# Down stage of a hybrid attention block: order of plain and seven-product groups, and the banks of the second block

## The chip, the cores and the metric

The kernel runs on one core of a Trainium2 chip. The metric is the device time of one execution in microseconds (us), the median of several runs. A profile of one execution goes with it. PE is TensorE (matmuls), PEld its weight loads, DVE is VectorE, ACT is ScalarE, POOL is GpSimd, SP is SyncE, which here only issues DMAs.

## The reference

One layer of a transformer block on 256 tokens of width 2048, all in float32. Three attention branches, their gated sum and a projection come first; then a feed-forward part. The change touches only the last product, the "down" product:

```python
h2 = rms_norm(x, g_ffn[l])
u = causal_depthwise_conv(h2 @ w_up[l], conv_w[l], conv_b[l])
u_gate, u_val = jnp.split(u, 2, axis=-1)
x = x + (jax.nn.silu(u_gate) * u_val) @ w_down[l]
```

The activations are 256 x 5632 and `w_down` is 5632 x 2048.

## The kernel before

**Three passes for one product.** Every float32 operand is held as a high part and a low remainder (`hi`, `lo`). A product of two such operands is three matmuls (`three`, lines 927 to 930): high by high, low by high, high by low. For the weights, ACT makes `hi` by a copy that rounds (L923), and DVE makes `lo` by a subtraction (L924), in `parts`. There are four `hi` and four `lo` buffers, so a piece of weights can be split only when the piece four earlier has been used up by PE.

**The down stage.** The 2048 output columns are done in two blocks of 1024 (`nb` 0 and 1). In each, the 5632 inner rows are 44 chunks of 128, taken two at a time as 22 groups, numbered `p`. The output of a block is 2 row halves (`t`) by 2 column halves of 512 (`n`), so four accumulators of one PSUM bank each, called `X`. A group is done in one of two ways:

- A plain group, "e" in the plan, function `eight`: eight products of 128 x 128 by 128 x 512, that is 24 matmuls, all into `X`. It takes two steps, one for each chunk. The last group of a block defers its matmuls to its second step and does them accumulator by accumulator (`close`), so that the first accumulator is final 18 matmuls before the last.
- A group by seven products, "s" in the plan, function `seven`: a two by two block product formed with seven products instead of eight, that is 21 matmuls. It takes four steps (`u0` to `u3`). Three products go into `X`, four go into four more accumulators called `Y`, one bank each. It needs sums of the activations (`forms`, lines 882 to 904) and sums of the weights. One part of the weight sums is made during the up stage by `weight_sums` (four loads of 256 KB, three additions on DVE, one write of 512 KB to a scratch tensor `T`, for each seven group); the other is made on the spot by two DVE additions (L985, L986).

After the last seven group of a block, `gather` adds the four `Y` in the right combinations to the residual tiles `xr` (eight DVE additions and one ACT copy, in three portions, the first held back by two further steps). After the block's last step, `finish` issues whatever of `gather` is still open, and `results` adds the four `X` banks to `xr` (L1059) and stores them (L1060).

**The order of the work.** `PLANS` holds one string for each block. In every step the program first issues the preparation of the step two ahead (loads, `hi`, `lo`), then the matmuls of this step, then what was put behind the step, and then one `tick` of the generators (`forms`, `gather`). The DVE, ACT and SP instructions that matter are pinned in this order (`keep`). The activation sums for group number `p` of the sevens are begun by a plain group: in the first block the fourth plain group begins the sums for seven number 0, the fifth those for number 1, and so on; in the second block this goes on from the second plain group. Their three portions are issued behind the plain group's first step, its second step and the step after it.

**The banks.** The first block takes its eight accumulators as four pairs from the pool `pp2` of the up stage. `start(1)` closes that pool and opens `pp3` with eight single banks. The variables `pairs_made`, `first_pair` and `turn_by` rotate the list of these eight before the first four become `X` and the last four `Y`. A bank is tied to a tile at the tile's first use, in the order of first use, and a fresh pool gives out its places from 0 downwards and round: 0, 7, 6, 5, 4, 3, 2, 1. In the program as compiled, the first block's `X` are in banks 0, 1, 6, 7 and its `Y` in 2, 3, 4, 5; the second block's `X` are in 0, 7, 6, 5 and its `Y` in 4, 3, 2, 1. Two tiles of a pair become free together, when both have been read for the last time.

## Time and profile before

| | us |
|---|---|
| median of 3 runs | 1492.92 |
| lowest, highest | 1491.57, 1492.92 |
| the profiled execution | 1492.96 |
| its span, first to last instruction | 1491.0 |

| part of the span | from, to (us) | PE busy | DVE busy | ACT busy | DMA, GB/s |
|---|---|---|---|---|---|
| attention, projections, nearly all of the up stage | 0 to 1250 | 1247.67 | 831.54 | 723.33 | 216 |
| end of the up stage | 1250 to 1256 | 6.00 | 2.63 | 2.34 | 238 |
| first block of the down stage | 1256 to 1372 | 114.69 | 107.40 | 72.17 | 246 |
| second block of the down stage | 1372 to 1491 | 114.18 | 99.19 | 61.74 | 234 |

Between the span and the profiled execution's own time lie 1.96 us. [...] The profile has one value for the clock that TensorE was granted, by stretch of time.

### The profile page before, as it was taken

Reading aid. Unit: us, or ns where it says so; the run is one execution under the profiler, and the core shown is the slowest. Engines: PE = TensorE matmul, PEld = TensorE weight load, DVE = VectorE, ACT = ScalarE, POOL = GpSimd, SP = SyncE. Lnnn points to the kernel's source line nnn. Section 1 sums busy time; section 2 is a strip of 40 time slices with the busy share of each in tenths; the row PEclk is TensorE's granted clock in tenths of the full one; section 3 lists DMA queues with packets and bytes.
Section 4 is the critical chain, followed back from the end, with each engine's and each line's share of the span. In section 5 each row is a group of like instructions: output and inputs, shape, how many; then the busy total and the mean of one; then the engine's idle time right before and its main releaser. Section 6 shows DMA issues by size and latency. Waiting matters only on the chain. (4 is left out here: it accounts for less than half of the span.)

```text
span 1491.0 us, 20205 instructions
## 1 busy us (share of the span) xinstructions
PE 1482.5 (99%) x7411; PEld 1250.9 (84%) x7411; DVE 1040.8 (70%) x1336; ACT 859.6 (58%) x1227; POOL 40.5 (3%) x90
## 2 busy tenths in 40 slices
PE   9999999999999999999999999999999999999998
PEld 7888888888888888888888888888888888887887
DVE  5767566555655646556556887777787787998987
ACT  6755454458544444444456676676676677564654
POOL 1000000001000000000000000000000000001000
PEclk9999999999999999999999999999999999999999
DMA  8675475475676667666677778778877885777874
GB/s 292 187 206 156 128 225 156 120 232 149 191 201 201 194 202 209 193 192 201 211 215 225 246 252 278 244 252 281 259 253 265 267 258 181 243 269 244 284 262 166
DMA packets 155939, 327.70 MB, mean 220 GB/s; under 512 B 11360, under 2 KB 19856, under 8 KB 155840
## 3 DMA queue, kind: packets, MB, share of 16 engines
q1 hardware_dynamic: 150496, 309.95, 66.8%
q0 software_dynamic: 4592, 15.41, 2.9%
q8 instruction: 58, 0.95, 0.3%
q10 hardware_dynamic: 752, 1.06, 0.2%
q14 instruction: 41, 0.34, 0.1%
HBM read 312.21 MB, written 14.16 MB: 219 GB/s over the span
## 5 line engine op out<-in xcount | busy, mean ns | idle before, releaser
L841 PE MATMUL u<-hT,hi_u 128*128 128x512 f32 x1408 | 442.4, 396 | 0.1
L843 PEld LDWEIGHTS u<-hT,lo_u 128*128 128x128 f32 x1408 | 264.4, 188 | 62.8 <-DVE lo_u L147 0.3
L843 PE MATMUL u<-hT,lo_u 128*128 128x256 f32 x1408 | 276.8, 278 | 0.0
L147 DVE TENSOR_TENSOR lo_u<-raw_u,hi_u 128x1024 fp32r<-128x1024 f32 x176 | 212.1, 1220 | 80.3 <-ACT hi_u L146 78.1
L146 ACT CAST hi_u<-raw_u 128x1024 fp32r<-128x1024 f32 x176 | 180.9, 1048 | 115.6 <-DMA raw_u<-in_w_up_dram 58.8
L841 PEld LDWEIGHTS u<-hT,hi_u 128*128 128x128 f32 x1408 | 214.3, 189 | 0.5 <-issue 0.5
L147 DVE TENSOR_TENSOR lo_g<-raw_g,hi_g 128x1024 fp32r<-128x1024 f32 x96 | 117.6, 1227 | 101.4 <-ACT hi_g L146 97.6
L146 ACT CAST hi_g<-raw_g 128x1024 fp32r<-128x1024 f32 x96 | 100.8, 1052 | 121.8 <-PE g L158 98.2
L157 PE MATMUL g<-hi_g,xT 128*128 128x512 f32 x384 | 150.9, 393 | 0.0
L159 PE MATMUL g<-lo_g,xT 128*128 128x512 f32 x384 | 149.6, 390 | 0.0
L158 PE MATMUL g<-hi_g,xT 128*128 128x512 f32 x384 | 149.5, 389 | 0.0
L159 PEld LDWEIGHTS g<-lo_g,xT 128*128 128x128 f32 x384 | 72.1, 188 | 15.2
L157 PEld LDWEIGHTS g<-hi_g,xT 128*128 128x128 f32 x384 | 72.1, 188 | 14.6
L158 PEld LDWEIGHTS g<-hi_g,xT 128*128 128x128 f32 x384 | 72.2, 188 | 14.5
L928 PE MATMUL d<-hi_d,aT 128*128 128x512 f32 x200 | 78.6, 393 | 2.0 <-DVE xr L1059 2.0
L930 PE MATMUL d<-lo_d,aT 128*128 128x512 f32 x200 | 78.5, 392 | 0.0
L929 PE MATMUL d<-hi_d,aT 128*128 128x512 f32 x200 | 78.4, 392 | 0.0
L772 DVE TENSOR_TENSOR y<-y,z 128x512 f32<-128x512 f32 x88 | 60.6, 690 | 20.2 <-ACT z L771 16.7
L771 ACT ACTIVATE z<-u,taps 128x256 f32<-128x256 f32 x176 | 74.7, 496 | 0.0
L147 DVE TENSOR_TENSOR lo_s<-raw_s,hi_s 128x1024 fp32r<-128x1024 f32 (+1 forms) x40 | 44.7, 1118 | 37.2 <-ACT hi_s L146 37.1
L147 DVE TENSOR_TENSOR lo_f<-raw_f,hi_f 128x1024 fp32r<-128x1024 f32 (+1 forms) x40 | 44.7, 1119 | 34.5 <-ACT hi_f L146 33.0
L146 ACT CAST hi_f<-raw_f 128x1024 fp32r<-128x1024 f32 (+1 forms) x40 | 38.6, 968 | 52.3 <-PE f L158 47.6
(332 smaller groups left out, 2801.0 us busy)
## 6 DMA issues: line engine op xcount, KB each, us to landing
raw_u<-in_w_up_dram SPq DMA_DIRECT2D x176, 512.0 KB, 4.6
raw_g<-in_w_in_dram SPq DMA_DIRECT2D x96, 512.0 KB, 4.0
raw_d<-in_w_down_dram SPq DMA_DIRECT2D x50, 512.0 KB, 5.1
r<-in_w_down_dram SPq DMA_DIRECT2D x76, 256.0 KB, 6.2
raw_s<-in_w_down_dram SPq DMA_DIRECT2D x38, 512.0 KB, 5.2
raw_f<-in_w_in_dram SPq DMA_DIRECT2D x32, 512.0 KB, 3.7
raw_s<-in_w_in_dram SPq DMA_DIRECT2D x32, 512.0 KB, 3.7
raw_o<-in_w_out_dram SPq DMA_DIRECT2D x32, 512.0 KB, 4.7
```

Of the source, the lines that this page charges most:

```text
L146: pin(nc.scalar.copy(hi[:, :m], raw[:, :m]))
L147: pin(nc.vector.tensor_tensor(lo[:, :m], raw[:, :m], hi[:, :m].bitcast(F32), ALU.subtract))
L157: nc.tensor.matmul(o, lhsT=xh, rhs=wh, start=first, stop=False)
L158: nc.tensor.matmul(o, lhsT=xl, rhs=wh, start=False, stop=False)
L159: nc.tensor.matmul(o, lhsT=xh, rhs=wl, start=False, stop=last)
L771: nc.scalar.activation(z[:, i], u[:, i, j : j + S], AF.Copy, scale=taps_of(j, i))
L772: nc.vector.tensor_tensor(y, y, z, ALU.add)
L841: nc.tensor.matmul(ps, lhsT=hi[:, j, c], rhs=hT[:, k + j, :], start=first, stop=False)
L843: nc.tensor.matmul(ps[:, :S], lhsT=lo[:, j, c], rhs=hT[:, k + j, :S], start=False, stop=last)
L928: nc.tensor.matmul(o, lhsT=ah, rhs=w[0], start=first, stop=False)
L929: nc.tensor.matmul(o, lhsT=al, rhs=w[0], start=False, stop=False)
L930: nc.tensor.matmul(o, lhsT=ah, rhs=w[1], start=False, stop=last)
```

## The change

Four things in the down stage:

1. The first block's plan keeps its 8 seven groups and 14 plain groups but orders them differently: two seven groups are drawn forward, and three plain groups in a row end the block.
2. The second block's plan has 12 seven groups and 10 plain groups, where it had 11 and 11. Four times two seven groups stand next to each other, and one plain group less lies between.
3. The rotation of the bank list is gone. In its place `start(1)` writes one column of the tiles 4, 5 and 6 with DVE, which are the second block's `Y[0]`, `Y[1]` and `Y[2]`.
4. `start` is called at other places in the program's text; the order in which it runs relative to `finish` and `results` stays.

With one more seven group `NSEVEN` becomes 8 and 12, so `weight_sums` runs 20 times during the up stage instead of 19.

```diff
-PLANS = ("eeeee" + "se" * 7 + "see", "e" + "se" * 4 + "sse" + "se" * 3 + "ssee")
+PLANS = ("eeeee" + "se" * 5 + "sse" + "s" + "eee", "e" + "se" * 3 + "sse" * 4 + "see")
...
-    pairs_made = [0]
-
     def two_banks(name):
-        pairs_made[0] += 1
         return pp2[0].tile([P, 2, 512], F32, tag="pair", name=name)
...
-    banks, first_pair = {}, [0]
+    banks = {}
 
     def start(nb):
         if nb == 0:
-            first_pair[0] = pairs_made[0] % 4
             pairs = [two_banks(f"d{nb}_{i}") for i in range(4)]
             b = [pair[:, i] for pair in pairs for i in range(2)]
         else:
             pp2x.close()
             pp3 = ctx.enter_context(tc.tile_pool(name="pp3", bufs=8, space=bass.MemoryType.PSUM, reuse_waits="tile"))
             b = [pp3.tile([P, 512], F32, tag="bank", name=f"d{nb}_{i}") for i in range(8)]
-            turn_by = 2 * first_pair[0] + 4
-            b = [b[(turn_by + i) % 8] for i in range(8)]
+            for i in (4, 5, 6):
+                keep(nc.vector.memset(b[i][:, :1], 0.0))
         banks[nb] = [[b[2 * t + n] for n in range(2)] for t in range(NT)], b[4:]
...
-        at(len(steps) - 1, lambda nb=nb: start(nb))
+        if nb == 0:
+            at(-1, lambda: start(0))
...
         at(len(steps) - 1, lambda nb=nb: results(nb))
+        if nb == 0:
+            at(len(steps) - 1, lambda: start(1))
```

## The prediction

> **What bounds the kernel now.** I read the page first, then what PE waited for, then the timeline around those waits.

> ```profile
> span 1491.0 us, 20205 instructions
> ...
> PE 1482.5 (99%) x7411; PEld 1250.9 (84%) x7411; DVE 1040.8 (70%) x1336; ACT 859.6 (58%) x1227; POOL 40.5 (3%) x90
> ```

> PE has work in 99% of the span, so a change can gain in two ways: fewer matmuls, or less of the little time that PE stands or runs slowly. The list of PE's waits has three rows; the longest (us in total, times, longest) is the only one in the down stage:

> ```profile
> PE d L928 <- DVE xr L1059: 2.0, 1, 2.0
> ```

> PE waits for `results` of the first block (L1059). The timeline at that place, PE first, then DVE (start, length, instruction, idle time before it and what ended it):

> ```profile
> 1369.63 0.39 PE L930 MATMUL d<-lo_d,aT 128*128 128x512 f32 x1
> ...
> 1370.31 0.39 PE L930 MATMUL d<-lo_d,aT 128*128 128x512 f32 x1
> 1372.68 0.47 PE L928 MATMUL d<-hi_d,aT 128*128 128x512 f32 x1 [1.99 <-DVE xr L1059]
> ...
> 1373.78 0.80 PE L928 MATMUL d<-hi_d,aT 128*128 128x512 f32 x1
> 1374.38 0.63 PE L929 MATMUL d<-hi_d,aT 128*128 128x512 f32 x1
> 1374.81 0.63 PE L930 MATMUL d<-lo_d,aT 128*128 128x512 f32 x1
> ...
> 1376.99 0.39 PE L930 MATMUL d<-lo_d,aT 128*128 128x512 f32 x1
> ```

> ```profile
> 1367.29 0.68 DVE L1027 TENSOR_TENSOR f<-e,d 128x512 f32<-128x512 f32 x1
> ...
> 1370.65 0.69 DVE L1033 TENSOR_TENSOR xr<-xr,e 128x512 f32<-128x512 f32 x1
> 1371.26 2.47 DVE L1059 TENSOR_TENSOR xr<-xr,d 128x512 f32<-128x512 f32 x4
> ```

> Three things are to be seen. First, PE's pace: from 1369.63 to 1370.31 are three starts, 0.68 us, so 0.2267 us for a matmul. Second, where the wait comes from. The last six additions of `gather` (1367.29 to 1371.34) stand on DVE ahead of the four of `results`, though the first accumulator was final 18 matmuls (4.1 us) before the end. The first matmul of the second block starts when two of the four results are through, and the fourth matmul, the first one into the second accumulator, starts at 1373.78, when all four are (1371.26 + 2.47 = 1373.73). So the second block accumulates on banks of the first block's `X`: the rotation missed. Third, after the wait the starts lie 0.43 us apart (1374.38 to 1374.81). The same stretch in windows of 2 us (length, busy us and count of PE, PEld, DVE, ACT and POOL, granted clock, DMA share, GB/s):

> ```profile
> 1370.00:1372.00 2.00, 0.69 (x4) 0.23 (x2) 1.97 (x4) 1.49 (x2) 0.00 (x0) 1.00 0.29 107
> 1372.00:1374.00 2.00, 1.32 (x4) 0.72 (x5) 2.00 (x4) 0.00 (x0) 1.63 (x3) 0.78 0.35 129
> 1374.00:1376.00 2.00, 2.00 (x5) 1.61 (x6) 2.00 (x4) 0.00 (x0) 0.98 (x2) 0.50 0.90 307
> 1376.00:1378.00 2.00, 2.00 (x9) 1.56 (x8) 0.67 (x2) 0.81 (x1) 1.18 (x3) 0.87 1.10 191
> ```

> The granted clock goes 1.00, 0.78, 0.50, 0.87. If it was 0.50 or 1.00 at any moment, it was halved for 0.88 + 2 + 0.52 = 3.4 us, right behind a wait of 2 us.

> **The change part by part.** *The end of the first block.* From 1370.31 to 1376.99 are 12 starts in 6.68 us; at pace they take 12 x 0.2267 = 2.72. The place costs 3.96 us: 2.14 of waiting (1370.31 to 1372.68, less one pace) and 1.82 of slow matmuls and the second wait. With three plain groups after the last seven group, the portions of `gather` go out in the second and third of them, each behind a `lo` split. DVE then has six splits of 1.14 us (their pace, below) and eight additions of 0.68 (six took 4.05), 12.3 us, in 3 x 24 x 0.2267 = 16.3 us of PE: nothing of `gather` stands before `results` at the end. The first three results come before the last matmul, and the fourth follows it, as at the end of the kernel now:

> ```profile
> 1486.47 0.39 PE L930 MATMUL d<-lo_d,aT 128*128 128x512 f32 x1
> 1486.90 0.75 DVE L1059 TENSOR_TENSOR xr<-xr,d 128x256 f32<-128x256 f32 x2 [0.67 <-PE d L930]
> ```

> PE need not wait even for these. The three small writes are the first uses of the new tiles, so by the order of handing out they get banks 0, 7 and 6, which are the first block's `X`; the new `X` get 5, 4, 3 and 2, all of the old `Y`, and these are free when `gather` ends. I take the whole 3.96 us as gained. The writes are new on DVE; no row shows one of 128x1, so each costs between 0 and the 0.29 us of the 128x128 addition below (L896); I take 0.1, the operand being much smaller. Behind them waits the split for the first seven group, which PE needs only after the first plain group (24 matmuls, 5.4 us); without that cover they would cost at most 0.9.

> *One more seven group.* 24 matmuls become 21: 3 x 0.2267 = 0.68 us less. DVE gets more: a seven group has three splits of 1024, one of 512 and two additions, a plain one two splits, and the extra sums are seven small operations. The cycle "se" with sums shows these in one row:

> ```profile
> 1297.00:1347.00 50.00, 50.00 (x223) 41.38 (x222) 49.52 (x76) 31.50 (x41) 0.00 (x0) 1.00 0.75 255
> ```

> DVE is busy 49.52 of 50 us while PE never waits: level, with nothing to spare. In the second block the sums end early, and "sse" without them takes, at paces of 1.14 and 0.60 (four of L1059 in 2.47, the last 0.68), two times 5.22 and 2.28, 12.7 us of DVE in 66 x 0.2267 = 15.0 of PE. That hides. In the up stage one more `weight_sums` comes in, at about 1206 to 1230, four loads, three additions of the shape of L1027 above (0.68) and one write:

> ```profile
> 1206.00:1228.00 22.00, 22.00 (x129) 19.20 (x128) 17.48 (x21) 15.62 (x24) 2.30 (x5) 1.00 0.85 268
> ```

> DVE has 4.5 us free in it, and PE does not wait: nothing. If DVE had no room there, it would be 2.0 us.

> *The denser first block.* The plan has "sse" and then "s". The sums for that last seven group are begun by the "e" just before it; in the old plan a whole "se" lies between. Their last DVE operation (L904) must be through before the eighth matmul of that group. The DVE chain, from rows of the one "sse" that ran (its first "s" starts at the PE row) and of a cycle with sums:

> ```profile
> 1420.74 0.39 PE L928 MATMUL d<-hi_s,aT 128*128 128x512 f32 x1
> ```

> ```profile
> 1423.88 1.23 DVE L924 TENSOR_TENSOR lo_s<-raw_s,hi_s 128x1024 fp32r<-128x1024 f32 x1 [0.21 <-ACT hi_s L923]
> ...
> 1428.65 2.35 DVE L924 TENSOR_TENSOR lo_d<-raw_d,hi_d 128x1024 fp32r<-128x1024 f32 x2
> 1430.92 1.98 DVE L924 TENSOR_TENSOR lo_s<-raw_s,hi_s 128x512 fp32r<-128x512 f32 x2
> ```

> ```profile
> 1339.01 0.68 DVE L924 TENSOR_TENSOR lo_s<-raw_s,hi_s 128x512 fp32r<-128x512 f32 x1
> ...
> 1341.32 0.29 DVE L896 TENSOR_TENSOR fr<-fr,rbc 128x128 f32<-128x128 f32 x1
> 1341.53 1.22 DVE L924 TENSOR_TENSOR lo_s<-raw_s,hi_s 128x1024 fp32r<-128x1024 f32 x1
> ...
> 1345.48 0.28 DVE L904 TENSOR_TENSOR aT<-fr,aT 128x128 fp32r<-128x128 f32 x1
> ```

> (The pair of splits from 1428.65 to 1430.92 gives the 1.14.) From the first "s": 3.14 until the second one's `lo` of 1024 begins, 7.04 from there to the `lo` of 512 of the third, 2.52 to its `lo` of 1024, 4.23 to the end of L904: 16.93 us. PE comes to that matmul after 21 + 21 + 24 + 7 = 73 matmuls, 16.55 us. It waits 0.4 us. The chain is joined from three places, so I take 0 and twice that, 0.8, as bounds. If so short a wait slowed the clock as the 2 us did, 1.8 us more would go; at a fifth of the idle time I don't count on it, but the range takes it in.

> The sum: 3.96 + 0.68 - 0.42 = 4.2 us. Against the profiled execution (1492.96, span 1491.0 and 1.96 around it), that is 1488.7; the median of the three runs, 1492.92, is the same within 0.04.

> **The rivals.**
> - *Loads late.* "sse" takes eight loads of 512 KB in 15.0 us, 4.19 MB or 280 GB/s, four times over. Against it: a stretch of the second block moved as much, and PE did not wait:

> ```profile
> 1430.00:1461.00 31.00, 31.00 (x138) 25.67 (x137) 24.48 (x26) 17.52 (x19) 0.00 (x0) 1.00 0.81 281
> ```

>   If single loads still come late by some 0.5 us in each of the four, 2.0 us go: 1490.7. Chance 0.10.
> - *Slower: the DMA engines become the bound there.* From the point where the rate held over these 60 us falls under 16.8 MB / 64.2 us = 261 GB/s, the gain is eaten. The DMA view of the down stage (1256 to the end) has:

> ```profile
> DMA packets 15943, 56.37 MB, mean 240 GB/s; under 512 B 1829, under 2 KB 2085, under 8 KB 15928
> ```

>   At such a rate the stretch takes 70 us, 10 more: 1498.7. For it speaks only that mean; against it the 281 above at a share of 0.81. Chance 0.04.
> - *The banks are not as said.* If a new `X` lies on the bank of the last result, PE waits for the fourth addition: 0.43 to its start and 0.68 for it, less one pace, about 0.9: 1489.6, and with the half clock again (1.8) 1491.4. Chance 0.07; even then `gather` is out of the way.
> - *The slow clock had another cause.* Then only the waits go, 2.14 and about 0.5: 4.2 - 1.3 = 2.9 us, 1490.1. Chance 0.04, since the clock is full before and falls at the wait. [...]

> **How the numbers follow.** The forecast has 0.75. A measurement of this kernel can tell about 0.2% (3.0 us, 1489.9) from no change. The runs before spread by 1.35 us, and the forecast lies 1.2 under that line, so I give 0.68 of its 0.75 to faster, 0.07 to within; with parts of the bank and clock cases faster is 0.72, within 0.24, slower 0.04. The range goes from 1487.4 (no wait for the sums, 1488.3, and 0.9 of spread) to 1490.8, which takes in the late loads and the slowed clock in the first block (1490.5).

> **What would show it.** PE's list of waits has no L1059, and the starts at the seam of the blocks stay 0.23 apart with the clock at 1.00. Instead a wait of some 0.4 us on DVE stands in the first block's last seven group, on L904. PE has three matmuls fewer in the down stage. Wrong would be: a clock under 1 in the down stage, waits of PE for `hi` or `lo` pieces in the second block, or for L1059.

## The result and the profile after

| | before | after |
|---|---|---|
| median, us (7 runs each, side by side) | 1492.92 | 1488.21 |
| lowest, highest | 1491.57, 1493.89 | 1487.89, 1489.44 |
| the profiled execution | 1492.96 | 1488.21 |
| its span | 1491.0 | 1486.5 |
| first to last matmul start of the down stage | 230.21 | 226.12 |

The ratio of the times is 0.9972, with an interval of 0.996 to 0.9983: a gain of 0.28%, small but clear of 1. The last row of the table is worked out from the timelines (1256.27 to 1486.47 before, 1255.67 to 1481.79 after), and the experiments below are read by it, since it leaves out what happens ahead of the down stage. Of the 4.75 us between the two profiled executions, 4.09 lie in it. 0.60 lie ahead of it, where the program after has one more `weight_sums`, which can't make it faster; the profiled executions of the experiments began the down stage anywhere between 1254.91 and 1256.35, whatever their plans, so this is the spread of single executions. What is left lies behind the last matmul and around the span.

In the listing after the change the lines of the down stage have moved: L925, L926, L927 are the three matmuls (before L928 to L930), L921 is `lo` (L924), L901 the last operation of the activation sums (L904), L1055 is `results` (L1059), L1043 the new small writes.

The page of after, its first lines:

```profile
span 1486.5 us, 20239 instructions
...
PE 1479.5 (100%) x7408; PEld 1248.4 (84%) x7408; DVE 1047.6 (70%) x1353; ACT 860.4 (58%) x1231; POOL 40.9 (3%) x91
```

Three matmuls fewer (7411 before), and DVE has 6.8 us more to do. PE's list of waits (us in total, times, longest) has one row of the down stage, the third:

```profile
PE spare L101 <- DVE qscale L251: 1.2, 1, 1.2
PE kv L159 <- DVE lo_kv L147: 0.5, 1, 0.5
PE d L926 <- DVE aT L901: 0.3, 1, 0.3
PE mT L186 <- DMA memres<-in_mem_dram: 0.2, 1, 0.2
```

The wait of 2.0 us for `results` is gone, and a short one for the sums of a seven group has come. The seam of the two blocks in PE's timeline (start, length, instruction), then in windows of 2 us (busy us and count of PE, PEld, DVE, ACT, POOL, then granted clock, DMA share, GB/s):

```profile
1370.27 0.39 PE L927 MATMUL d<-lo_d,aT 128*128 128x512 f32 x1
1370.49 0.39 PE L925 MATMUL d<-hi_d,aT 128*128 128x512 f32 x1
1370.72 0.39 PE L926 MATMUL d<-hi_d,aT 128*128 128x512 f32 x1
```

```profile
1370.00:1372.00 2.00, 2.00 (x10) 1.65 (x10) 1.30 (x3) 1.46 (x2) 0.51 (x2) 1.00 0.99 303
1372.00:1374.00 2.00, 2.00 (x11) 1.65 (x10) 1.99 (x6) 0.81 (x1) 1.14 (x3) 1.00 0.80 315
1374.00:1376.00 2.00, 2.00 (x11) 1.65 (x10) 2.00 (x3) 0.29 (x2) 1.26 (x4) 1.00 0.89 186
```

The rows are 0.39 us long and start 0.22 and 0.23 us apart, so the pace is read from the starts. The first block's last matmul starts at 1370.27 and the second block's first at 1370.49, one pace later; the clock stays at 1.00. DVE at the same place:

```profile
1366.32 0.69 DVE L1030 TENSOR_TENSOR xr<-xr,e 128x512 f32<-128x512 f32 x1
...
1368.06 1.28 DVE L1055 TENSOR_TENSOR xr<-xr,d 128x512 f32<-128x512 f32 x2
1370.69 1.29 DVE L1055 TENSOR_TENSOR xr<-xr,d 128x512 f32<-128x512 f32 x2 [1.35 <-PE d L927]
1371.98 0.13 DVE L1043 MEMSET d<- 128x1 f32 x3
```

`gather` ends at 1367.01 (1366.32 + 0.69), 3.3 us ahead of the last matmul. Only a split (L921, 1.22 us) stands between it and the first two results. The last results end at 1371.98, 1.7 us after the last matmul's start, and PE doesn't wait for them: the new `X` lie on banks that `gather` had emptied.

### The profile page after: what moved, and what is told of

It is laid out like the page before. It is cut to its first block, busy times and chain, and to the rows that moved or that the text cites. A ratio compares the mean times of both kernels' runs of the same rounds, so it can differ in the third digit from the quotient of the medians.

```text
span 1486.5 us, 20239 instructions
## 1 busy us (share of the span) xinstructions
PE 1479.5 (100%) x7408; PEld 1248.4 (84%) x7408; DVE 1047.6 (70%) x1353; ACT 860.4 (58%) x1231; POOL 40.9 (3%) x91
## 4 chain that ended last, share of the span: by engine, by line
PE 96%; ACT 1%; DVE 1%; DMA 1%; issue 1%; POOL 0%; SPq 0%; DVEq 0%; POOLq 0%; ACTq 0%
PE u L838 22%; PE u L840 11%; PE g L157 5%; PE g L159 5%; PE g L158 5%; PE d L926 5%; PE d L927 5%; PE d L925 5%; PE s L157 2%; PE s L159 2%; PE f L157 2%; PE f L159 2%; PE f L158 2%; PE s L158 2%; PE b L157 2%; PE b L159 2%
## 5 line engine op out<-in xcount | busy, mean ns | idle before, releaser
L925 PE MATMUL d<-hi_d,aT 128*128 128x512 f32 x192 | 74.7, 389 | 0.0
L926 PE MATMUL d<-hi_d,aT 128*128 128x512 f32 x192 | 74.7, 389 | 0.0
L927 PE MATMUL d<-lo_d,aT 128*128 128x512 f32 x192 | 74.7, 389 | 0.0
```

Of the source, the lines that this page charges most:

```text
L925: nc.tensor.matmul(o, lhsT=ah, rhs=w[0], start=first, stop=False)
L926: nc.tensor.matmul(o, lhsT=al, rhs=w[0], start=False, stop=False)
L927: nc.tensor.matmul(o, lhsT=ah, rhs=w[1], start=False, stop=last)
```

## The experiments

The theory: the seam costs what it costs because the new `X` lie on banks that are read last, behind `gather`; the waiting (1.99 us) halves the clock for 3.4 us; take that away and 3.96 us go, the seven group saves 0.68 and its early sums take back some 0.4. Against it stood that one part of the change does nearly all, or that the clock has a cause of its own. All kernels below compute the reference in full; e6 and e9 only add copies that nobody uses.

| kernel | median of n, us | before beside it | ratio and interval | down stage, us |
|---|---|---|---|---|
| e1_banks | 1488.83 (9) | 1492.49 (26) | 0.9976 [0.9966, 0.9986] | 226.56 |
| e2_plan0 | 1490.05 (11) | 1492.49 | 0.9986 [0.9977, 0.9995] | 227.80 |
| e3_seven | 1491.93 (11) | 1492.49 | 0.9996 [0.9987, 1.0005] | 229.85 |
| e4_order | 1487.90 (6) | 1492.49 | 0.9971 [0.996, 0.9983] | 225.54 |
| e5_late_banks | 1489.87 (10) | 1492.17 (33) | 0.9986 [0.9977, 0.9995] | 227.84 |
| e6_later_banks | 1491.40 (10) | 1492.17 | 0.9995 [0.9986, 1.0004] | 228.45 |
| e7_spread | 1490.22 (10) | 1492.17 | 0.9985 [0.9976, 0.9995] | 228.13 |
| e8_thirteen | 1488.48 (11) | 1492.17 | 0.9978 [0.9969, 0.9987] | 226.32 |
| e9_three_copies | 1493.99 (10) | 1491.76 (22) | 1.0012 [1.0003, 1.0021] | 231.14 |
| e10_changed_again | 1488.47 (9) | 1491.76 | 0.9976 [0.9966, 0.9985] | 226.12 |
| e11_order_again | 1487.65 (8) | 1491.76 | 0.9973 [0.9962, 0.9983] | 225.54 |

### The three parts, each alone

**The banks alone** (e1_banks): `start(1)` of the change, with the plans of before (the diff is shortened: the counters of the rotation and the places of the calls of `start` are also those of the change).

```diff
-            turn_by = 2 * first_pair[0] + 4
-            b = [b[(turn_by + i) % 8] for i in range(8)]
+            for i in (4, 5, 6):
+                keep(nc.vector.memset(b[i][:, :1], 0.0))
```

> The kernel before with the new banks alone (both old plans; the memsets in place of the rotation). My theory: the new accumulators lie on the old Y banks, whose last reader is the seventh of the eight gather additions (it ended at 1370.61 in the trace of before, where the next matmul was due at 1370.54). So PE waits about 0.15 to 0.2 us at the seam instead of 2.1, the clock stays full, and of the 3.96 us of the seam about 3.75 go although gather is as late as it was: about 1489.2 against 1492.9. Rival: what frees the seam is the order of the groups, which takes gather out of the way; with the old order PE goes on waiting for DVE and the time stays at 1492.9.

The down stage took 226.56 us, 3.65 less than before. `gather` and `results` still stand late on DVE, but PE doesn't need the results any more. PE's timeline of e1, then DVE's:

```profile
1369.40 0.39 PE L927 MATMUL d<-lo_d,aT 128*128 128x512 f32 x1
1369.85 0.47 PE L925 MATMUL d<-hi_d,aT 128*128 128x512 f32 x1
1370.16 0.40 PE L926 MATMUL d<-hi_d,aT 128*128 128x512 f32 x1
```

```profile
1369.02 0.69 DVE L1029 TENSOR_TENSOR e<-e,d 128x512 f32<-128x512 f32 x1
1369.74 0.69 DVE L1030 TENSOR_TENSOR xr<-xr,e 128x512 f32<-128x512 f32 x1
1370.35 2.47 DVE L1055 TENSOR_TENSOR xr<-xr,d 128x512 f32<-128x512 f32 x4
```

The second block starts at 1369.85, half a microsecond before the first of the four results. All that is left is 0.31 us: the starts are 0.45 and 0.31 apart, where the pace is 0.2267. The first matmul comes 0.14 us after `gather`'s last reading of a `Y` (L1029, to 1369.71). So the banks alone give nearly the whole gain of the seam.

**The first plan alone** (e2_plan0): three plain groups end the first block, with the banks of before.

```diff
-PLANS = ("eeeee" + "se" * 7 + "see", "e" + "se" * 4 + "sse" + "se" * 3 + "ssee")
+PLANS = ("eeeee" + "se" * 5 + "sse" + "s" + "eee", "e" + "se" * 4 + "sse" + "se" * 3 + "ssee")
```

> The kernel before with the new first plan alone (old second plan, old rotated banks). My theory: gather is out of the way, three of the four results come before the last matmul, and only the fourth is waited for by the first matmul into the second accumulator: about 0.3 us there, with a full clock, and the 0.5 us in the last seven group. So 3.96 - 0.3 - 0.5 = 3.2 us go: about 1489.7. Rival: the banks decide; with them wrong PE waits about 0.9 us for the fourth result and the clock is halved again (1.8 us): 1491.5 to 1492.

227.80 us, only 2.41 less, and the seam still has a wait. (Of the 1.55 us that are left over pace, 0.55 are the wait for the early sums, which the plan brings with it, and 1.00 the seam, at full clock.) PE's waits of e2, in the down stage, and its timeline at the seam, then DVE's (lines as before the change):

```profile
PE d L928 <- DVE xr L1059: 0.7, 1, 0.7
PE d L929 <- DVE aT L904: 0.3, 1, 0.3
```

```profile
1369.51 0.39 PE L930 MATMUL d<-lo_d,aT 128*128 128x512 f32 x1
...
1370.19 0.39 PE L930 MATMUL d<-lo_d,aT 128*128 128x512 f32 x1
1371.28 0.50 PE L928 MATMUL d<-hi_d,aT 128*128 128x512 f32 x1 [0.70 <-DVE xr L1059]
```

```profile
1369.94 1.28 DVE L1059 TENSOR_TENSOR xr<-xr,d 128x512 f32<-128x512 f32 x2 [1.35 <-PE d L930]
```

The first block ends with the matmul at 1369.51. Three matmuls of the second block run, and the fourth, the first into the second accumulator, waits for the fourth result (to 1371.22). I had expected 0.3 us at the seam, because the third accumulator was final six matmuls before the end, and its result should have been through by then. DVE shows otherwise: it stood idle for 1.35 us and began the third result at 1369.94, 0.43 after the last matmul, and the fourth right behind it. Both tiles are halves of one pair of the old pool. They were read only when the pair's last matmul was done. The clock stays full (1.00 in the five windows of 2 us from 1368 to 1378), so the rival, a wait of 0.9 us with a halved clock, was near in the wait alone.

The end of the changed kernel shows the same order of work on single banks. DVE first, then PE's last matmul:

```profile
1480.85 0.69 DVE L1055 TENSOR_TENSOR xr<-xr,d 128x512 f32<-128x512 f32 x1 [0.67 <-PE d L927]
```

```profile
1481.79 0.39 PE L927 MATMUL d<-lo_d,aT 128*128 128x512 f32 x1
```

There the third result starts at 1480.85, 0.43 us after its own accumulator's last matmul (six starts before 1481.79, at 1480.42), and doesn't wait for the fourth accumulator.

**The seven group alone** (e3_seven): the second plan of the change, all else as before.

```diff
-PLANS = ("eeeee" + "se" * 7 + "see", "e" + "se" * 4 + "sse" + "se" * 3 + "ssee")
+PLANS = ("eeeee" + "se" * 7 + "see", "e" + "se" * 3 + "sse" * 4 + "see")
```

> The kernel before with the new second plan alone (12 seven groups; old first plan, old rotated banks). My theory: three matmuls fewer, 0.68 us, and nothing else; the seam keeps its wait of 2 us and its half clock, no new wait of PE in the second block, the up stage with 20 weight sums as long as with 19: about 1492.2. Rival: the extra sums on DVE, the extra loads and the denser sevens cost PE something, and the time is 1492.9 or more.

229.85 us, 0.36 less where 0.68 was expected, and the time can't be told from no change. PE got no new wait in the second block, and the three matmuls are gone; but the seam cost 4.29 us in this execution and not 3.96. Its windows show the half clock later than before the change:

```profile
1372.00:1374.00 2.00, 1.72 (x6) 1.16 (x7) 2.00 (x4) 0.00 (x0) 1.83 (x4) 0.93 0.55 201
1374.00:1376.00 2.00, 2.00 (x7) 1.54 (x6) 2.00 (x3) 0.00 (x0) 0.66 (x2) 0.50 0.94 320
1376.00:1378.00 2.00, 2.00 (x8) 1.62 (x7) 0.41 (x2) 1.05 (x1) 1.03 (x3) 0.71 1.00 129
```

Before the change it was 0.78, 0.50, 0.87: less of it lay in the first window and more in the third. In both it lasted 3.41 us, but in e3 it lay wholly in matmuls, and before partly in the second wait.

### Is it the wait that halves the clock, and how long must it be?

**The new `X` on the banks read last** (e5_late_banks): of the change only one tile is written, so that the new `X` get banks 7, 6, 5 and 4. Then e6_later_banks and e9_three_copies hold the last result up by one and by three copies on DVE. The edit shown is that of e9; e6 has one copy without the loop, and e5 has the first two lines alone.

```diff
-            for i in (4, 5, 6):
+            for i in (4,):
...
+                    if (nb, t, n) == (0, 1, 1):
+                        for _ in range(3):
+                            z = sm.tile([P, 512], F32, tag="junk", bufs=2, name="delay")
+                            keep(nc.vector.tensor_copy(z, banks[0][0][1][0]))
```

> The changed kernel with one small write instead of three, so the second block's accumulators get banks 7, 6, 5 and 4: the first two were the last pair of the first block. My theory, with the dependency kept for a pair as a whole: the third and the fourth result start 0.43 us after the last matmul's start and one behind the other (0.60), the fourth ends 1.7 us after it, and the first matmul of the second block waits until then: 1.77 from start to start, 1.54 more than the pace. Down stage 226.12 + 1.54 = 227.7 us from first to last matmul start, if an idle time of 1.4 us leaves the clock full; 229.4 if it halves it for 3.4 us. Rival: each bank is a dependency of its own and only the fourth result waits for the last matmul: 0.9 more, 227.0.

> The same as e5_late_banks with one DVE copy of 128x512 put ahead of the fourth result, into a scratch tile that nothing reads: 0.60 us more of idle time for PE, 2.0 us in all, as long as in the kernel before. My theory: the idle time sets the clock, so it is halved for 3.4 us behind it, though the plans and gather are those of the changed kernel: 227.7 + 0.6 + 1.7 = 230.0 us for the down stage. Rival: the half clock of the kernel before came from something else at that place (the late gather, the loads that bunched); then the clock stays full and the down stage takes 228.3.

> e6_later_banks with three DVE copies instead of one ahead of the fourth result: PE idles 3.3 us at the seam instead of 2.1. In e6_later_banks the clock stayed full in the profiled execution, while in the kernel before and in e3_seven a wait of 2.0 us was followed by 3.41 us at half clock. My theory: the clock is judged in stretches of 3.41 us that run on without regard to the program; it is halved for one such stretch when PE idled for more than about half of the one before, so a wait of 2 us does it or not by where it falls (1.98 and 1.78 us in one stretch did, 1.60 and 1.47 did not), and 3.3 us nearly always does it. Then the down stage takes 228.45 + 1.2 + 1.7 = 231.4 us, and the time is about 1493.4. Rival: the half clock of the kernel before came from something that the changed kernel doesn't have; then the clock stays full with any wait: 229.7 and about 1491.7.

PE's timeline at the seam, e5 first, then e6, then e9:

```profile
1369.89 0.39 PE L927 MATMUL d<-lo_d,aT 128*128 128x512 f32 x1
1371.74 0.47 PE L925 MATMUL d<-hi_d,aT 128*128 128x512 f32 x1 [1.47 <-DVE d L1043]
```

```profile
1370.59 0.39 PE L927 MATMUL d<-lo_d,aT 128*128 128x512 f32 x1
1373.05 0.47 PE L925 MATMUL d<-hi_d,aT 128*128 128x512 f32 x1 [2.07 <-DVE d L1043]
1373.36 0.40 PE L926 MATMUL d<-hi_d,aT 128*128 128x512 f32 x1
1373.59 0.39 PE L927 MATMUL d<-lo_d,aT 128*128 128x512 f32 x1
```

```profile
1370.13 0.39 PE L927 MATMUL d<-lo_d,aT 128*128 128x512 f32 x1
1373.78 0.77 PE L925 MATMUL d<-hi_d,aT 128*128 128x512 f32 x1 [3.26 <-DVE d L1043]
1374.34 0.63 PE L926 MATMUL d<-hi_d,aT 128*128 128x512 f32 x1
```

The waits were 1.47, 2.07 and 3.26 us. The profile names the small write L1043 as what ended them; it stands on DVE right behind the last result, and in the changed kernel, where the `X` lie elsewhere, the first matmul doesn't wait for it. e5 fits what was expected (227.84 against 227.7). In e6 the theory missed for this execution: PE waited 2.07 us, longer than the 1.99 of before the change, and the starts behind it are at full pace, 0.23 apart. In e9 they are 0.43 and more apart, and its 231.14 us fit the 231.4 expected, not the 229.7 of the rival. The windows of e6, then of e9:

```profile
1372.00:1374.00 2.00, 0.95 (x4) 0.85 (x5) 2.00 (x5) 0.00 (x0) 0.90 (x2) 1.00 0.83 330
1374.00:1376.00 2.00, 2.00 (x10) 1.65 (x10) 1.88 (x3) 0.17 (x1) 1.79 (x4) 1.00 0.50 135
```

```profile
1372.00:1374.00 2.00, 0.22 (x1) 0.26 (x2) 2.00 (x5) 0.00 (x0) 0.62 (x2) 0.88 0.57 227
1374.00:1376.00 2.00, 2.00 (x5) 1.58 (x6) 2.00 (x4) 0.00 (x0) 1.61 (x3) 0.50 0.45 160
1376.00:1378.00 2.00, 2.00 (x8) 1.59 (x7) 0.61 (x2) 0.00 (x0) 0.00 (x0) 0.76 0.89 277
```

So the wait does halve the clock here (3.26 us in e9, 1.99 us before the change), but its length isn't all that decides (2.07 us in e6 left it full). What else went with it stands in the last section. e9 also shows how much hangs on the bank: one held up so that PE waits 3.26 us makes the changed kernel slightly slower than the one before, with all else of the change in place (1.0012, 1.0003 to 1.0021).

**Accumulators spread over pairs** (e7_spread): e2 with each `X` paired with a `Y`, to take apart the pair and the single bank.

```diff
-            b = [pair[:, i] for pair in pairs for i in range(2)]
+            b = [pair[:, i] for i in range(2) for pair in pairs]
```

> e2_plan0 with the first block's accumulators dealt to the four pairs one by one (each X with a Y in a pair) instead of two X to a pair. In e2_plan0 PE waited 0.86 us at the seam for the fourth result. My theory: it waited because third and fourth result hang on the pair's last matmul; with the pairs dealt so, the first, second and third new accumulator lie on pairs whose result is through before the seam, and the fourth is used only 2.3 us behind it. No wait at the seam: 227.80 - 0.97 = 226.8 us for the down stage. Rival: any accumulator of the second block on an old X bank costs the wait, whatever the pairing: 227.8.

It missed both numbers: 228.13 us. Now `gather`, which reads `Y`, shares pairs with `X`, which still grows, so it ran late and took `results` with it. ACT's copy of `Y[0]` in e7, then DVE's timeline:

```profile
1360.81 0.59 ACT L1023 COPY e<-d 128x512 f32<-128x512 f32 x1 [2.58 <-PE d L930]
```

```profile
1370.08 1.22 DVE L924 TENSOR_TENSOR lo_d<-raw_d,hi_d 128x1024 fp32r<-128x1024 f32 x1
1371.21 1.88 DVE L1059 TENSOR_TENSOR xr<-xr,d 128x512 f32<-128x512 f32 x3
```

The run doesn't take pair and bank apart at the seam as it was meant to, but it does in another place. `Y[0]` was final with the last seven group, and behind that group the first block's matmuls write only `X`. Still its copy waited for a matmul (L930): it started 6.5 us behind the first matmul after the group (1354.27), in e2 3.9 us (1357.07 behind 1353.19). With the third result, late on a pair and early on a single bank, this shows the pair as the unit on which this program's instructions wait.

### Is there more in the plans?

**Another order in the first block** (e4_order, and once more beside the change as e11_order_again; e10_changed_again is the change): the plain group that begins the sums for the last seven group moves one seven group earlier.

```diff
-PLANS = ("eeeee" + "se" * 5 + "sse" + "s" + "eee", "e" + "se" * 3 + "sse" * 4 + "see")
+PLANS = ("eeeee" + "se" * 6 + "ss" + "eee", "e" + "se" * 3 + "sse" * 4 + "see")
```

> The changed kernel with another first plan: five plain groups, six times seven and plain, two sevens, three plain. The sums for the last seven group are begun one seven group earlier than in the changed kernel. My theory: the wait of 0.5 us in that group is owed to this one distance, so it goes and nothing takes its place: PE never waits in the down stage, about 0.5 us less than the changed kernel, 1487.7. Rival: DVE is level there whatever the order, so a wait of the same size shows up at another piece of the first block: 1488.2, as the changed kernel.

> The changed kernel once more, beside e11_order_again on the same chip: 1488.2 to 1488.6.

> e4_order once more, beside the changed kernel. By the down stages in the profiles (225.54 and 226.12 us) it is 0.6 us faster than that: 1487.6 to 1488.0. Rival: what is gained in the last seven group of the first block is lost in the spread of the rest, and the two are the same.

225.54 us, both times, against 226.12 of the change, both times. PE's list of waits of e4 has no row of the down stage any more; the last one is of the up stage:

```profile
PE u L838 <- DVE xres L716: 0.2, 1, 0.2
```

Beside each other the medians are 1487.65 and 1488.47. The 0.58 us are shown by the traces; the times of the two agree with them, though their intervals against the kernel before overlap. It is the fastest version that ran.

**A thirteenth seven group** (e8_thirteen), on top of e4.

```diff
-PLANS = ("eeeee" + "se" * 6 + "ss" + "eee", "e" + "se" * 3 + "sse" * 4 + "see")
+PLANS = ("eeeee" + "se" * 6 + "ss" + "eee", "e" + "sse" * 5 + "se" + "ssee")
```

> e4_order with one more seven group in the second block: 13 sevens and 9 plain, plan e, five times sse, se, ssee. My theory: DVE and the four pairs of hi and lo buffers are now the limit; three matmuls fewer give 0.68 us, but in the five times two sevens with the sums of five more groups among them PE waits some 0.4 us three times for the lo part of the T piece; together 0.6 us longer than e4_order: 226.1 for the down stage, about 1488.5. Rival: DVE keeps up as it did with 12, nothing waits, 0.68 us less: 224.9, about 1487.2.

226.32 us, 0.78 more than e4, though three matmuls fewer should have given 0.68 less. The size is near the 226.1 expected, but the piece that PE waits for is not the `lo` that was named. PE's timeline at the first of three such places with the weight load (PEld) of its second row, then DVE's and ACT's:

```profile
1412.71 0.39 PE L926 MATMUL d<-hi_t,aT 128*128 128x512 f32 x1
1413.18 0.50 PE L925 MATMUL d<-hi_t,sf 128*128 128x512 f32 x1
```

```profile
1413.18 0.19 PEld L925 LDWEIGHTS d<-hi_t,sf 128*128 128x128 f32 x1 [0.51 <-ACT hi_t L920]
```

```profile
1411.29 0.68 DVE L983 TENSOR_TENSOR t<-raw_s,raw_s 128x512 f32<-128x512 f32 x1
```

```profile
1412.08 1.05 ACT L920 CAST hi_t<-t 128x1024 fp32r<-128x1024 f32 x1 [2.42 <-DVE t L983]
```

The second DVE addition of the weight sum made on the spot ends at 1411.97. ACT, idle for 2.42 us until then, makes its `hi` until 1413.13, and PE starts at 1413.18. So DVE is late, and PE feels it through ACT. With activation sums still running, "sse" leaves DVE hardly a gap: from 1380 to 1450 it was busy 69.03 of 70 us in e8, 67.73 in e4. PE falls behind by 0.25 to 0.32 us, and 0.11 after it, at each of three such places, 1.2 us in all; the rest are starts some hundredths apart. In this order DVE has no room for a thirteenth seven group; other orders of thirteen were not tried.

## Why the prediction was right

- **The seam, 3.96 us: right, and gone entirely.** There is no gap at the seam and the clock is full (1.00). Two remedies went into it, of which one would nearly do: the banks alone took 3.65 of it, the first plan alone 2.96 (2.41 with the wait that this plan brings). The prediction had counted both together and didn't say which carries it.
- **The seven group, 0.68 us: right** in matmuls (7408), and nothing of it was lost: no wait for pieces in the second block, none in the up stage. "Loads late" and "DMA engines as the bound" did not happen.
- **The wait for the early sums: there, at 0.55.** The working gave 16.93 - 16.55 = 0.38; the sum took 0.42, which stands in no working and changes nothing that counts. It stands in the last seven group of the first block, on L901, as forecast:

```profile
1350.20 0.39 PE L925 MATMUL d<-hi_s,aT 128*128 128x512 f32 x1
1350.87 0.50 PE L926 MATMUL d<-hi_s,aT 128*128 128x512 f32 x1 [0.28 <-DVE aT L901]
1351.20 0.40 PE L927 MATMUL d<-lo_s,aT 128*128 128x512 f32 x1
```

  The gaps are 0.67 and 0.33, 0.44 and 0.11 over pace. It did not slow the clock (1.00 from 1255.6 to 1370). Together: 3.96 + 0.68 - 0.55 = 4.09, which is what the down stage shows. That the time came out 0.5 us under the forecast is chance: 0.60 us lie ahead of the down stage, in the spread of single executions.
- **The small writes: 0.13 us for three,** where 0.1 each was taken; hidden, as said.
- **Wrong in a detail: "the first three results come before the last matmul".** Two did. The third and fourth, halves of one pair, began 0.43 us after the last matmul's start (row of DVE above). It cost nothing here, as no new `X` lay on them. But it shows the rival "banks not as said" to have been priced too low: 0.9 us were given, and e5 measured 1.63 + 0.08.
- **The slow clock: right as a cause, too firm as a term.** Half clock stood behind the wait of 1.99 us before the change and behind the 3.26 us of e9, and with no wait the clock was full (1.00 after the change and in e4). The prediction took the half clock as part of the seam in every execution. Part of the executions of before don't have it, by their mean clock (last section), and then the seam costs less: e6 shows 2.23 + 0.08 us over pace for a wait of 2.07 at full clock. What the change is worth therefore depends on the runs of before it is set against: 4.71 us by the first medians, 3.29 beside e10. The kernel after, which has no such wait, repeats better (1487.64 to 1489.44 in 16 runs), and it is its time that was forecast.

## What to carry to other kernels

Where one set of accumulators follows another, find out which bank each new one gets and which reader empties it last: putting the first new accumulators on the banks emptied first took away 3.65 us without moving any work. Tiles cut from one two-bank allocation came free, and became readable, together in this program (in e2 the third result began 0.43 us after the pair's last matmul, six matmuls after its own accumulator was final). Here stalls of PE of about 2 us had 3.41 us of half clock behind them in some executions (1.99 us, before the change) and not in others (2.07 us, e6): price such a stall with both, and set the kernel without it against several sets of runs.

## What the runs showed of the hardware that was not expected

| kernel | idle of the wait, us | of it in one stretch | share | halved |
|---|---|---|---|---|
| e5 | 1.47 | 1.47 | 43% | no |
| e6 | 2.07 | 1.60 | 47% | no |
| e3 | 1.99 and 0.17 | 1.78 + 0.17 | 57% | yes |
| before | 1.99 | 1.99 | 58% | yes |
| e9 | 3.26 | 3.02 | 88% | yes |

In these five a stretch idle for 57% and more had half clock behind it, and one idle for 47% or less had none; a wait of 2 us went one way or the other by where it fell. PE also stops at the end of every kernel, and that gives more cases, with idle time counted, as in the table, from the end of a matmul's row (0.39 us after its start). Before the change, the stretch up to 1489.16 us has 2.30 us of idle time (67%), and the clock is 0.50 from there to the end of the span. After the change, the stretch up to 1483.87 us has 1.70 us of idle time (50%), and the next one stayed full. In e5, e8 and e11 a last stretch with 1.97 us (58%) was followed by half clock. In all 13 kept traces no stretch with up to 50% was followed by half clock, and each with 57% or more was, as far as the clock record goes. The wait wasn't moved along the grid on purpose, so what a stretch idle for between 50% and 57% brings was not measured.

**So the same program has two prices.** Each run lists its mean granted clock. Of the 81 runs of before beside the experiments, 34 had 0.998, and their times average 1492.6; 13 had 1.000, and they average 1491.2; on each of the three chips taken alone the first are slower by 1.1 to 1.6 us. e6 has both too: three runs of 0.998 average 1492.2, four of 1.000 average 1490.7. The kernels whose seam has no wait, or 0.31 us of it, never showed 0.998 (e10 and e1, 18 runs). Even with the 3.3 us of e9 one run of ten has 1.000, at 1491.84 against a median of 1493.99; by estimate, a wait of 3.26 us cut in two halves by the grid would leave 1.63 us, 48%, in each stretch, less than the 50% that had no half clock behind it. No execution of the kernel before with a full clock was traced, so that the half clock makes the difference between its two prices is argued from these numbers. Between 0.998 and 1.000 a mean clock can't be read, since the half clock at the end of the span (0.50 from 1489.16 to 1491.04 before the change) lowers it too.

**A write of 128x1 has a record of 0.06 us** on DVE in e5, where it stands alone, and three took 0.13 together after the change; the nearest row before was 0.29 for 128x128.
